# Nine matmuls on a zeroed tile at the start, and all tables loaded on the SP queue, in a two-layer encoder trunk

## The chip, the cores and the metric

The kernel runs on one core of a Trainium2 chip. The metric is the device time of one launch in microseconds. Engines work side by side, each with its own queue in order: PE multiplies matrices, PEld is its weight load, DVE and ACT work elementwise, POOL and SP mostly issue DMAs here. DMAs can be issued from SP, ACT and POOL.

## What is computed

Two layers over x (512 positions of 1024 channels, float32), then a final RMSNorm:

```python
for l in range(DEPTH):
    h = rms_norm(x, norm1_g[l])
    za, xb, q, k, v, g = jnp.split(h @ w_in[l], splits, axis=-1)
    ya = spatial_gating(jax.nn.gelu(za), a_vnorm_g[l], a_ws[l], a_bs[l])
    yb = multiscale_pool(xb, b_w[l], b_scale[l])
    yc = retention(q, k, v, g, c_norm_g[l])
    x = x + jnp.concatenate([ya, yb, yc], axis=-1) @ w_out[l]
    x = x + conv_ffn(rms_norm(x, norm2_g[l]), w_up[l], conv_w[l], conv_b[l], w_down[l])
return rms_norm(x, final_g)
```

The retention part uses rotary tables (cos, sin), a decay mask over pairs of positions and decay factors by head; the spatial gating uses a 128x128 weight per head with a block mask and a bias; the pooling uses one weight per group, its window counts and a selector.

## The kernel before

x stands transposed, eight tiles X[k] of 128 channels x 512 positions. Every float32 operand of a large matmul is split in two float32r halves, a rounded one (h) and the rest (l), and a product is three matmuls: h x h, h x l, l x h. ACT writes the h half (a cast or a scaled copy), DVE the l half (a subtraction).

The weights are cut on the host into 192 slots of 128 x 1024, 96 per layer, in the order in which PE uses them. The class Weights loads them on the SP queue into a ring of five raw tiles (wr) and splits them into rings of five tiles (wh, wl). The first four slots come in halves of 256 KB, each followed by one x row (Weights.first, lines 65 to 78); the others are single loads of 512 KB (line 83), asked for three slots ahead of use (line 91).

load_x (line 710) loads X[k] on SP and calls Norm.feed (line 171): a copy of the row scaled by the norm's gain (ACT, n_kh), its rest (DVE, n_kl), its square (ACT, n_kq) and the running sum of squares (DVE, into n_0q). For k = 0 a small square root follows, which brings an activation table load. The gains are columns of the vector table vecs; ACT's queue loads its first eight columns at k = 0 and the others at k = 3.

In mixing (line 246) the first projection is token_proj for the values, slots 0 to 3. Each x row k is one block of 12 matmuls: four groups of 128 positions, each h x h, h x l, l x h in that order (lines 241 to 243), so that the third matmul of a block is the first that needs n_kl. Before the last block the hook puts in the statistics (n_0ss: matmuls of the summed squares with ones), and behind the first two rows of the query projection (slot 4) the spreading of the norm factor (n_0rb). The order in which the many small steps of mixing are written out is the string MIX; the queues of all engines are ordered by a planner when the program is built, which may pull an instruction ahead of others of its engine.

The tables: selt, cntt, dmt, dect and epst (lines 133 to 143), loaded once, and wst, bit, bwt, cos and sin (lines 254 to 263), loaded for each layer, all issued from POOL. cos and sin take tiles from the ring U of 48 general tiles; wst, bit and bwt have one tile each, which layer 1 gets when layer 0 is done with it. Their first readers are late in the layer, but for dect and cos, which are read when the norm factor is there.

The up projections of layer 0's ffn end with slot 84, and slot 85 is the first of its last down projection.

Of the kernel before, what the change touches and what calls it, by code (L numbers as in the profile page):

```python
# [10 lines left out]
F32 = mybir.dt.float32  # L11
F32R = mybir.dt.float32r
# [4 lines left out]
P = 128  # L17
# [3 lines left out]
KT = D // P  # L21
NT = T // P
AW = 256
CW = 512
HEADS = 8
# [14 lines left out]
SLOTS_PER_LAYER = 96  # L40
LOOK = 3
FIN = 2
MIX = (
    "Q0 K0 v23 G0 v01 Q1 s0 K1 G1 s1 y0 Q2 s2 y1 K2 s3 B0 y2 Q3 s4 y3 K3 "
    "m0 r01 s5 y4 A s6 G2 y5 G3 s7 y6 y7 r2 c1 c0 B1 r3 a U1 c2 c3 m1 U0"
# [2 lines left out]
SLOT = {}  # L48
for _n in MIX:
    if _n[0] in "QKGBUA":  # L50
# [48 lines left out]
def trunk(ctx: ExitStack, tc: tile.TileContext, xT, wflat, vec, ws_t, bias_t, bw, rope, dmask, vdec, geps, cnt, sel, out):  # L99
    nc = tc.nc  # L100
    cp = ctx.enter_context(tc.tile_pool(name="const", bufs=1))
    lp = ctx.enter_context(tc.tile_pool(name="layer", bufs=1))
# [6 lines left out]
    def U(name, dt=F32, cols=T):  # L109
        return up.tile([P, cols], dt, tag="u", name=name)  # L110

    def PS(name):
        return psp.tile([P, T], F32, tag="ps", name=name)

    def f(ap):
        return ap.bitcast(F32)
# [9 lines left out]
    vecs = cp.tile([P, NV], F32, name="vecs")  # L126
# [4 lines left out]
    eps = cp.tile([P, 1], F32, name="eps")  # L131
    nc.vector.memset(eps, EPS)
    selt = cp.tile([P, 2], F32, name="selt")
    nc.gpsimd.dma_start(out=selt, in_=sel)
    cntt = cp.tile([P, 2, 17], F32, name="cntt")
    nc.gpsimd.dma_start(out=cntt, in_=cnt)

    dmt = cp.tile([P, HEADS, P], F32, name="dmt")
    nc.gpsimd.dma_start(out=dmt, in_=dmask)
    dect = cp.tile([P, NT, HEADS], F32, name="dect")  # L140
    nc.gpsimd.dma_start(out=dect, in_=vdec)
    epst = cp.tile([P, 4, NT, 2], F32, name="epst")
    nc.gpsimd.dma_start(out=epst, in_=geps)

    def rsqrt(src, n, scale, name, eps_t=None):
        m = sp.tile([P, n], F32, tag="rm", name=name + "m")
# [99 lines left out]
    def mixing(l, nm, nxt):  # L246
# [5 lines left out]
            return vecs[:, vc + c : vc + c + 1]  # L252

        wst = lp.tile([P, 4, P], F32, tag="wst", name=f"wst{l}")
        nc.gpsimd.dma_start(out=wst, in_=ws_t[l])
        nc.gpsimd.memset(wst[CHUNK:P, :, 0:CHUNK], 0.0)
        bit = lp.tile([P, 2, P], F32, tag="bit", name=f"bit{l}")
        nc.gpsimd.dma_start(out=bit, in_=bias_t[l])
        bwt = lp.tile([P, 2, P], F32, tag="bwt", name=f"bwt{l}")
        nc.gpsimd.dma_start(out=bwt, in_=bw[l])  # L260
        cosr, sinr = U(f"cos{l}"), U(f"sin{l}")
        nc.gpsimd.dma_start(out=cosr, in_=rope[0])
        nc.gpsimd.dma_start(out=sinr, in_=rope[1])

        vb = token_proj(f"v{l}_", base, 4, CW, hs, ls, nm.stats)
        V = []
# [264 lines left out]
        def step(name):  # L531
            kind, i = name[0], [int(c) for c in name[1:]]
            if kind == "Q":
                q(i[0])
            elif kind == "K":
                k(i[0])
            elif kind == "G":
                gate(i[0])
            elif kind == "v":
                v_center(i)  # L540
            elif kind == "s":
                scores(i[0])
            elif kind == "y":
                ymix(i[0])
            elif kind == "r":
                yvar(i)
            elif kind == "c":
                ycat(i[0])
            elif kind == "A":
                state["va"] = va_begin()  # L550
            elif kind == "B":
                state[i[0]] = pool(i[0])
            elif kind == "m":
                poolmap(i[0], state[i[0]])
            elif kind == "a":
                state["sg"] = spatial(state["va"])
            elif kind == "U":
                acat(i[0], state["sg"][i[0]])

        for name in MIX:  # L560
            step(name)

        ch, cl = [c[0] for c in cat], [c[1] for c in cat]
        place = {"c": 4, "m": 2, "U": 0}
        order = [place[n[0]] + int(n[1]) for n in MIX if n[0] in place]
        banks = {}
# [66 lines left out]
    def finish(s, G):  # L633
        def down(m, c, n, hook=None):
            ps = PS(f"fd{m}_{c.start}")[:, : c.stop - c.start]
            for k in range(FH):
                if k == 4 and hook is not None:
                    hook()
                i = m * FH + k
                mm3(ps, W.get(s + i // KT), i % KT, G[k][0][:, c], G[k][1][:, c], k == 0, k == FH - 1)  # L640
            nc.vector.tensor_tensor(out=X[m][:, c], in0=X[m][:, c], in1=ps, op=ALU.add)
            sq = U(f"fq{m}_{c.start}")[:, : c.stop - c.start]
            nc.scalar.activation(out=sq, in_=X[m][:, c], func=AF.Square)
            return sq
# [3 lines left out]
        nc.scalar.activation(out=warm, in_=total[:, :1], func=AF.Sqrt)  # L648
        for m in range(1, KT - FIN):
            sq = down(m, slice(0, T), T)  # L650
            nc.vector.tensor_tensor(out=total, in0=total, in1=sq, op=ALU.add)
        r = {}
        for th in range(2):
            c = slice(th * H, (th + 1) * H)
            part = total[:, c]
            for m in range(KT - FIN, KT):
                hook = None
                if th == 1 and m == KT - FIN:
                    sums = [part0, sq]
# [4 lines left out]
                sq = down(m, c, H, hook)  # L664
                if th == 1 and m == KT - FIN:
                    fin_out(0, r[0])
# [19 lines left out]
    def fin_out(th, r):  # L686
        rb = PS(f"frb{th}")
        for b in range(NT // 2):
            nc.tensor.matmul(
                rb[:, b * P : (b + 1) * P], r[:, b : b + 1].to_broadcast([P, P]), ident, start=True, stop=True  # L690
            )
        c = slice(th * H, (th + 1) * H)
        for k in range(0, KT, 2):
            o = U(f"fin{th}_{k}")
            for i in range(2):
                nc.vector.scalar_tensor_tensor(
                    out=o[:, i * H : (i + 1) * H],
                    in0=X[k + i][:, c],
                    scalar=vecs[:, C_FG + k + i : C_FG + k + i + 1],
                    in1=rb[:, :H],  # L700
                    op0=ALU.mult,
                    op1=ALU.mult,
                )
            (nc.sync if k % 4 else nc.scalar).dma_start(
                out=out[th, :, k : k + 2, :], in_=o.rearrange("p (a t) -> p a t", a=2)
            )
# [3 lines left out]
    def load_x(k):  # L710
        xt = cp.tile([P, T], F32, name=f"x{k}")
        nc.sync.dma_start(out=xt, in_=xT[k])
        if k == 0:
            nc.scalar.dma_start(out=vecs[:, :8], in_=vec[:, :8])
        if k == 3:
            nc.scalar.dma_start(out=vecs[:, 8:], in_=vec[:, 8:])
        X.append(xt)
        nm.feed(k)

    W.first(load_x)  # L720
    for l in range(DEPTH):
        n2 = Norm(f"n2_{l}", l * LC + C_N2)
        mixing(l, nm, n2)
        nm = Norm(f"n1_{l + 1}", (l + 1) * LC + C_N1) if l < DEPTH - 1 else None
        ffn(l, n2, nm)
# [106 lines left out]
```

## Time and profile before

| | us |
|---|---|
| median of three runs | 1141.26 (1140.46 to 1141.29) |
| span of the profiled execution, first to last instruction | 1139.3 |
| PE busy | 1125.2 (99%) |
| DVE busy | 746.4 (66%) |
| ACT busy | 525.1 (46%) |
| POOL busy | 27.5 (2%) |

The busy time of PE counts matmuls from start to a modelled end, so that it says where PE stands idle, not how fast it goes; how fast it goes is read from the distance between the starts of matmuls. The chain of work that ended last names, from the end back to the start, what each step waited for. The granted clock of PE is 0.998 of full speed as a mean of the span; the two levels are 1.2 and 2.4 GHz. Queue q1 is SP's, q10 ACT's and q0 POOL's.

### The profile page before, as it was taken

Reading aid. Unit: us, or ns where it says so; the run is one execution under the profiler, and the core shown is the slowest. Engines: PE = TensorE matmul, PEld = TensorE weight load, DVE = VectorE, ACT = ScalarE, POOL = GpSimd, SP = SyncE. Lnnn points to the kernel's source line nnn. Section 1 sums busy time; section 2 is a strip of 40 time slices with the busy share of each in tenths; the row PEclk is TensorE's granted clock in tenths of the full one; section 3 lists DMA queues with packets and bytes.
Section 4 is the critical chain, followed back from the end, with each engine's and each line's share of the span. In section 5 each row is a group of like instructions: output and inputs, shape, how many; then the busy total and the mean of one; then the engine's idle time right before and its main releaser. Section 6 shows DMA issues by size and latency. Waiting matters only on the chain.

```text
span 1139.3 us, 13715 instructions
## 1 busy us (share of the span) xinstructions
PE 1125.2 (99%) x5378; PEld 941.7 (83%) x5378; DVE 746.4 (66%) x1103; ACT 525.1 (46%) x731; POOL 27.5 (2%) x71
## 2 busy tenths in 40 slices
PE   8999999999999999999999999999999999999997
PEld 6888888888888888888888898888888888888886
DVE  6898676576763377764448877666777435777534
ACT  7577745444431244444327785534444213444420
POOL 2010000000000000000001000000000000000000
PEclk9999999999999999999999999999999999999999
DMA  9433222233223222233224322222232223322202
GB/s 326 146 111 93 75 75 96 90 102 102 93 93 101 103 93 93 97 105 113 93 93 123 100 74 71 78 93 93 96 107 94 93 96 106 95 93 93 93 1 74
DMA packets 33361, 112.83 MB, mean 99 GB/s; under 512 B 4320, under 2 KB 4496, under 8 KB 33296
## 3 DMA queue, kind: packets, MB, share of 16 engines
q1 hardware_dynamic: 29952, 103.82, 27.1%
q0 software_dynamic: 2480, 6.87, 2.3%
q10 hardware_dynamic: 864, 1.26, 0.3%
q8 instruction: 42, 0.69, 0.2%
q14 instruction: 23, 0.19, 0.0%
HBM read 105.64 MB, written 2.10 MB: 95 GB/s over the span
## 4 chain that ended last, share of the span: by engine, by line
PE 99%; DVE 0%; DMA 0%; ACT 0%; issue 0%; DVEq 0%; SPq 0%; ACTq 0%
PE up L214 14%; PE up L212 14%; PE up L213 14%; PE dn L214 5%; PE dn L213 5%; PE dn L212 5%; PE o L212 3%; PE o L214 3%; PE o L213 3%; PE fd L212 2%; PE fd L213 2%; PE fd L214 2%; PE v L241 1%; PE v L242 1%; PE v L243 1%; PE k L213 1%
## 5 line engine op out<-in xcount | busy, mean ns | idle before, releaser
L86 ACT CAST wh<-wr 128x1024 fp32r<-128x1024 f32 x188 | 197.7, 1052 | 291.7 <-PE dn L213 104.2
L87 DVE TENSOR_TENSOR wl<-wr,wh 128x1024 fp32r<-128x1024 f32 x188 | 229.8, 1223 | 106.0 <-ACT wh L86 103.1
L610 DVE SCALAR_TENSOR_TENSOR cc<-uu,vecs,cc 128x511 f32<-128x511 f32 (+1 forms) x176 | 131.4, 748 | 5.4 <-ACT cc L606 2.3
L606 ACT ACTIVATE cc<-uu,vecs 128x512 f32<-128x512 f32 x88 | 71.5, 815 | 7.9 <-DVE uu L604 7.7
L614 ACT ACTIVATE cc<-cc 128x512 f32<-128x512 f32 x44 | 27.8, 632 | 79.0 <-DVE cc L610 79.0
L604 DVE TENSOR_TENSOR uu<-up,n_1bc 128x512 f32<-128x512 f32 x44 | 30.2, 688 | 40.9 <-PE up L214 40.9
L604 DVE TENSOR_TENSOR uu<-up,n_0bc 128x512 f32<-128x512 f32 x44 | 30.2, 688 | 40.9 <-PE up L214 40.9
L626 DVE TENSOR_TENSOR x<-x,dn 128x512 f32<-128x512 f32 x24 | 16.5, 687 | 40.9 <-PE dn L214 40.9
L212 PE MATMUL up<-n_0h,wh 128*128 128x512 f32 x88 | 34.7, 394 | 0.0
L213 PE MATMUL up<-n_0l,wh 128*128 128x512 f32 x88 | 34.3, 390 | 0.0
L214 PE MATMUL up<-n_1h,wl 128*128 128x512 f32 x88 | 34.3, 390 | 0.0
L212 PE MATMUL up<-n_1h,wh 128*128 128x512 f32 x88 | 34.3, 390 | 0.0
L212 PE MATMUL up<-n_3h,wh 128*128 128x512 f32 x88 | 34.3, 390 | 0.0
L214 PE MATMUL up<-n_5h,wl 128*128 128x512 f32 x88 | 34.3, 390 | 0.0
L214 PE MATMUL up<-n_2h,wl 128*128 128x512 f32 x88 | 34.3, 390 | 0.0
L212 PE MATMUL up<-n_7h,wh 128*128 128x512 f32 x88 | 34.3, 390 | 0.0
L213 PE MATMUL up<-n_4l,wh 128*128 128x512 f32 x88 | 34.3, 390 | 0.0
L213 PE MATMUL up<-n_6l,wh 128*128 128x512 f32 x88 | 34.3, 390 | 0.0
L213 PE MATMUL up<-n_5l,wh 128*128 128x512 f32 x88 | 34.3, 390 | 0.0
L214 PE MATMUL up<-n_6h,wl 128*128 128x512 f32 x88 | 34.3, 390 | 0.0
L214 PE MATMUL up<-n_3h,wl 128*128 128x512 f32 x88 | 34.3, 390 | 0.0
L212 PE MATMUL up<-n_4h,wh 128*128 128x512 f32 x88 | 34.3, 390 | 0.0
(959 smaller groups left out, 3058.3 us busy)
## 6 DMA issues: line engine op xcount, KB each, us to landing
wr<-in_wflat_dram SPq DMA_DIRECT2D x188, 512.0 KB, 3.5
wr<-in_wflat_dram SPq DMA_DIRECT2D x8, 256.0 KB, 7.3
x<-in_xT_dram SPq DMA_DIRECT2D x8, 256.0 KB, 7.8
qs_0h<-qs_0h POOLq DMA_DIRECT2D x8, 128.0 KB, 2.3
qs_1h<-qs_1h POOLq DMA_DIRECT2D x8, 128.0 KB, 3.7
qs_0l<-qs_0l POOLq DMA_DIRECT2D x8, 128.0 KB, 3.4
qs_1l<-qs_1l POOLq DMA_DIRECT2D x8, 128.0 KB, 3.8
out_dram<-fin ACTq DMA_DIRECT2D x4, 256.0 KB, 2.2
```

The lines of the kernel that those rows point to most:

```text
L86: nc.scalar.copy(hi, src)
L87: nc.vector.tensor_tensor(out=lo, in0=src, in1=hi.bitcast(F32), op=ALU.subtract)
L212: nc.tensor.matmul(ps, hi[:, k, :], xh, start=first, stop=False)
L213: nc.tensor.matmul(ps, hi[:, k, :], xl, start=False, stop=False)
L214: nc.tensor.matmul(ps, lo[:, k, :], xh, start=False, stop=last)
L241: nc.tensor.matmul(o, hs[k][:, bs], hi[:, kk, :], start=k == 0 and b % pack == 0, stop=False)
L242: nc.tensor.matmul(o, hs[k][:, bs], lo[:, kk, :], start=False, stop=False)
L604: nc.vector.tensor_tensor(out=u, in0=ps, in1=nm.bc, op=ALU.mult)
L606: nc.scalar.activation(out=c, in_=u, func=AF.Identity, scale=w[2], bias=vecs[:, vc + C_CB + t : vc + C_CB + t + 1])
L610: nc.vector.scalar_tensor_tensor(out=c[:, d:], in0=u[:, : T - d], scalar=w[2 - d], in1=c[:, d:], op0=ALU.mult, op1=ALU.add)
L614: nc.scalar.activation(out=c, in_=c, func=AF.Silu)
L626: nc.vector.tensor_tensor(out=X[m], in0=X[m], in1=ps, op=ALU.add)
```

## The change

A tile of 128 x 512 is zeroed by DVE, and nine matmuls of its first 128 columns with the whole tile write a PSUM tile that nothing reads. The DMAs of all tables go from POOL to SP: the five that are loaded once stand in layer 0 behind cos and sin, and so behind the 16 weight and x rows of Weights.first. The order within a layer is now cos, sin, (the five), bwt, bit, wst. The larger part of vecs goes from ACT at the fourth x row to SP at the last.

```diff
+WARM = 9
@@
     selt = cp.tile([P, 2], F32, name="selt")
-    nc.gpsimd.dma_start(out=selt, in_=sel)
     cntt = cp.tile([P, 2, 17], F32, name="cntt")
-    nc.gpsimd.dma_start(out=cntt, in_=cnt)
-
     dmt = cp.tile([P, HEADS, P], F32, name="dmt")
-    nc.gpsimd.dma_start(out=dmt, in_=dmask)
     dect = cp.tile([P, NT, HEADS], F32, name="dect")
-    nc.gpsimd.dma_start(out=dect, in_=vdec)
     epst = cp.tile([P, 4, NT, 2], F32, name="epst")
-    nc.gpsimd.dma_start(out=epst, in_=geps)
+
+    zero = U("zero", F32R)
+    nc.vector.memset(f(zero), 0.0)
+    busy = PS("busy")
+    for i in range(WARM):
+        nc.tensor.matmul(busy, zero[:, :P], zero, start=True, stop=True)
+
+    def load_tables():
+        for t, src in ((dect, vdec), (selt, sel), (cntt, cnt), (epst, geps), (dmt, dmask)):
+            nc.sync.dma_start(out=t, in_=src)
@@
         wst = lp.tile([P, 4, P], F32, tag="wst", name=f"wst{l}")
-        nc.gpsimd.dma_start(out=wst, in_=ws_t[l])
+        bit = lp.tile([P, 2, P], F32, tag="bit", name=f"bit{l}")
+        bwt = lp.tile([P, 2, P], F32, tag="bwt", name=f"bwt{l}")
+        cosr, sinr = U(f"cos{l}"), U(f"sin{l}")
+        nc.sync.dma_start(out=cosr, in_=rope[0])
+        nc.sync.dma_start(out=sinr, in_=rope[1])
+        if l == 0:
+            load_tables()
+        nc.sync.dma_start(out=bwt, in_=bw[l])
+        nc.sync.dma_start(out=bit, in_=bias_t[l])
+        nc.sync.dma_start(out=wst, in_=ws_t[l])
         nc.gpsimd.memset(wst[CHUNK:P, :, 0:CHUNK], 0.0)
-        bit = lp.tile([P, 2, P], F32, tag="bit", name=f"bit{l}")
-        nc.gpsimd.dma_start(out=bit, in_=bias_t[l])
-        bwt = lp.tile([P, 2, P], F32, tag="bwt", name=f"bwt{l}")
-        nc.gpsimd.dma_start(out=bwt, in_=bw[l])
-        cosr, sinr = U(f"cos{l}"), U(f"sin{l}")
-        nc.gpsimd.dma_start(out=cosr, in_=rope[0])
-        nc.gpsimd.dma_start(out=sinr, in_=rope[1])
@@
-        if k == 3:
-            nc.scalar.dma_start(out=vecs[:, 8:], in_=vec[:, 8:])
+        if k == KT - 1:
+            nc.sync.dma_start(out=vecs[:, 8:], in_=vec[:, 8:])
```

## Rows read from the trace of the kernel before

**Rows 1.** Waits of PE: waiter, releaser: us in total, times, longest.

```profile
PE v L241 <- ACT n_0h L176: 5.6, 1, 5.6
PE frb L689 <- DVE fr1r L162: 1.3, 1, 1.3
```

**Rows 2.** The chain that ended last, its start: start us, us, what.

```profile
1.19 3.55 DMA x<-in_xT_dram
4.82 0.73 ACT n_0h L176
5.60 0.80 PE v L241
...
10.23 0.43 PE v L242
...
10.93 0.23 PE v L241
```

**Rows 3.** Stretches: length, busy (instructions) by engine, granted clock, DMA share, GB/s.

```profile
5.60:10.60 5.00, 5.00 (x12) 3.86 (x13) 2.17 (x3) 3.44 (x6) 0.68 (x5) 1.00 1.00 348
10.60:16.00 5.40, 5.40 (x25) 4.46 (x24) 4.41 (x7) 4.68 (x9) 1.37 (x3) 1.00 1.05 382
```

**Rows 4.** Timeline of PE: start us, us, line, operation [idle before <- releaser].

```profile
6.19 0.63 PE L242 MATMUL v<-wl,n_0h 128*128 128x512 f32 x1
...
13.98 0.39 PE L243 MATMUL v<-wh,n_2l 128*128 128x512 f32 x1
...
27.13 0.95 PE L193 MATMUL n_0ss<-ones,n_0q 128*128 128x1 f32 x8
...
30.80 0.39 PE L212 MATMUL q<-n_0h,wh 128*128 128x512 f32 x1
...
507.63 0.39 PE L212 MATMUL dn<-G_11h,wh 128*128 128x512 f32 x1
```

**Rows 5.** Timeline of DVE.

```profile
0.84 0.06 DVE L132 MEMSET eps<- 128x1 f32 x1
...
12.27 0.75 DVE L177 SCALAR_TENSOR_TENSOR n_2l<-x,vecs,n_2h 128x512 fp32r<-128x512 f32 x1
...
25.33 0.69 DVE L187 TENSOR_TENSOR n_0q<-n_0q,n_7q 128x512 f32<-128x512 f32 x1
...
56.58 0.17 DVE L368 MEMSET sc<- 128x128 f32 x1
```

**Rows 6.** DMA queues, 2 to 4 us (q10), then 6 to 12 us.

```profile
q10 hardware_dynamic: 229, 0.14, 23.3%
...
q1 hardware_dynamic: 590, 1.08, 52.4%
q0 software_dynamic: 407, 1.09, 49.5%
```

**Rows 7.** Timeline of ACT.

```profile
8.28 0.72 ACT L176 ACTIVATE n_1h<-x,vecs 128x512 fp32r<-128x512 f32 x1 [0.97 <-DMA x<-in_xT_dram]
9.02 1.28 ACT L185 ACT_TABLE_LOAD   x1
...
14.57 0.60 ACT L75 CAST wh<-wr 128x512 fp32r<-128x512 f32 x1
...
16.22 0.60 ACT L75 CAST wh<-wr 128x512 fp32r<-128x512 f32 x1
...
21.63 1.05 ACT L86 CAST wh<-wr 128x1024 fp32r<-128x1024 f32 x1 [0.18 <-DMA wr<-in_wflat_dram]
...
23.12 0.71 ACT L176 ACTIVATE n_7h<-x,vecs 128x512 fp32r<-128x512 f32 x1
```

**Rows 8.** Timeline of POOL, the table loads of layer 1.

```profile
149.40 0.57 POOL L255 DMA_DIRECT2D wst<-in_ws_t_dram  x1 [43.79 <-PE sg L500]
...
512.73 0.54 POOL L262 DMA_DIRECT2D cos<-in_rope_dram  x1 [354.19 <-DVE cc L616]
513.76 0.54 POOL L263 DMA_DIRECT2D sin<-in_rope_dram  x1 [0.50 <-DVE G_21l L122]
```

**Rows 9.** Timeline of SP, 0 to 512.7 us: the weight loads in it.

```profile
14.26 496.01 SPq L83 DMA_DIRECT2D wr<-in_wflat_dram  x91
```

**Rows 10.** DMA issues on the page: KB each, median us to landing.

```profile
wr<-in_wflat_dram SPq DMA_DIRECT2D x188, 512.0 KB, 3.5
```

## The prediction

> **What bounds the kernel now.** I read the waits of the PE first: it waited 5.6 us for its first operand and after that only at the very end [rows 1]. Everything between is one line of matmuls, and the page gives the chain of the end 99% to PE. So a change pays only by what it takes off PE's own line, and here that is the start. Second, the chain from time zero [rows 2]: weight row, x row (landed at 1.19 + 3.55 = 4.74), ACT's scaled copy, first projection matmul at 5.60. The next matmuls on the chain stand 0.43 us apart up to 10.23 and 0.23 us apart from 10.93. In the table of stretches twelve matmuls lie between 5.60 and 10.60, twenty-five between 10.60 and 16.00 [rows 3]. The fine paces: 0.427 us slow, which is 512 columns at the 1.2 GHz level, and 0.227 fast (58 matmuls from 13.98 to 27.13 [rows 4]). The clock column says 1.00 in both stretches, but the pace is nearly halved. I trust the pace and put the rise at 10.55, that is 4.95 us after PE's first matmul. Third, how late PE is against its supply in the first projection: the third matmul of a block needs the low half of x (n_kl on DVE), and it runs 0.96 us after that for block 2 (12.27 + 0.75 = 13.02 against 13.98 [rows 4, 5]); the stats matmuls at 27.13 run 1.1 us after their sum (25.33 + 0.69 = 26.02 [rows 4, 5]).
>
> **The change, step by step.** Its own time is the span, 1139.3 us; the median of the runs, 1141.26, lies 1.96 us above it, and I carry that over.
>
> *Nine matmuls added.* They need only a DVE memset of 128x512, behind two small ones that end at 0.90 [rows 5]. Its price is not in the trace: below, a 128x128 memset took 0.17 us, above, a DVE pass over 128x512 took 0.69 [rows 5]. From 0.06 for one column and 0.17 for 128 I estimate 0.06 + 511 x 0.11/127 = 0.50 us, so it ends near 1.4 and the first added matmul starts there. In the profile the second matmul starts 0.59 after the first (6.19 against 5.60), the others 0.43 apart [rows 2, 4]. Nine at the slow pace occupy PE to 1.4 + 0.59 + 8 x 0.427 = 5.4. That is idle time of PE until 5.60 [rows 1]; what is left of it is what matters. If the memset takes 0.69, they end at 5.6 and delay nothing against before.
>
> *First real operand.* In 2 to 4 us ACT's queue (q10, the rest of the vector table) had 23.3% of the DMA time [rows 6]. Moved behind the x rows, it frees up to 0.23 x 2 = 0.5 us: x row 0 lands near 4.25 and the first real matmul could start at 5.05 to 5.60. It stands behind the nine until 5.4, so I take 5.4: 0.2 us earlier.
>
> *The clock.* If the rise comes 4.95 us after the first matmul as in this profile, it comes at 1.4 + 4.95 = 6.35. From 5.4 to 6.35 some 2.2 real matmuls are slow instead of 12. Each slow one costs 0.427 - 0.227 = 0.20. Block 0 (12 matmuls) ends at 5.4 + 12 x 0.227 + 2.2 x 0.20 = 8.6. Before, it ended at 10.7 [rows 2]. Gain 2.1 us. Bounds: rise before 5.0, block 0 from 5.1 (with 0.2 lost to n_0l) ends at 8.0, gain 2.7; rise two us later than I put it, four more slow matmuls, gain 1.3; no earlier rise than 10.55, gain 0.2.
>
> *The tables leave POOL's queue.* In 6 to 12 us they (q0) had 49.5% of the DMA time and SP's rows 52.4% [rows 6]. ACT waited for x row 1 until 8.28 [rows 7]. Behind the rows, 256 KB each take about 0.67 us at 385 GB/s (382 between 10.6 and 16 [rows 3]): row 1 lands near 4.25 + 2 x 0.67 = 5.6, row 7 near 13.6. Then ACT and DVE set the supply: ACT's passes for one row take 1.65 us (from the weight cast at 14.57 to the next at 16.22), and an activation table load of 1.28 stands before block 2's copy [rows 7]. Row 0's copy ends near 5.0; one round later, with 0.5 allowed for landings, n_1h is there at 7.15 and, with DVE's 0.75 [rows 5], n_1l at 7.9, against the third matmul of block 1 at 8.6 + 0.45 = 9.05. The table load and another round give n_2h at 10.1 and n_2l at 10.9, against 11.8. PE needs 2.72 per block, ACT 1.65, so the margin grows. Without this move the early clock would be worth only the 0.96 us of margin above: both parts are needed.
>
> *What the move puts on SP.* Eleven more issues before slot 4 (the first 512 KB load), at most the 0.57 us that an issue on POOL took [rows 8], 6 us in all, and some 1.8 MB, 4.7 us at 385 GB/s, which run at the same time. Slot 4 is used by the query projection at 30.80 [rows 4]; 6.5 MB up to and with it take 17 us at 382 GB/s; from a first landing near 3 that is 20, so this is hidden. Of the tables, dect and cos are read first, behind the statistics at 27.13, so later than slot 4 lands; dmt first by the score stage, whose memset stands at 56.58 [rows 4, 5]. ACT loses one issue and POOL ten; PE, which waited for nothing between [rows 1], did not wait for them either. POOL's memset of wst waits longer; behind it on POOL stand only the copies of the first query tile, which come after the projection that starts at 30.80.
>
> *Layer 1.* Five issues now stand between weight loads on SP, where before POOL waited 354.19 us for cos and 43.79 us for wst [rows 8]. SP had issued 91 loads (slots 4 to 94) by 512.7, while PE was in slot 85 [rows 4, 9]: nine slots, some 49 us, of cover. I cost it at nothing; without cover see the last rival.
>
> Sum: -0.2 (start) - 1.9 (ten slow matmuls at 0.20, less rounding) = -2.1: span 1137.2, time 1139.2. PE has no wait after 5.60 that could swallow it before the tail [rows 1], and the tail moves with it.
>
> **The rivals.**
>
> *The rise comes early.* The clock is up before the first real matmul: no slow ones are left, gain 2.7, 1138.6. For it: nothing shows that the delay of 4.95 us is fixed. Against: it is the only delay this trace shows. The Trainium skill ("TensorE: Matmul & The Clock Gate", section "What's actually happening") says that one kernel showed 6, 11 and 14 slow matmuls at its start in different runs. No two profiles here show that; by it the gain would scatter to both sides of mine. It would also make the time before scatter, and the three runs do, by 0.8 us.
>
> *The nine do not lift the clock earlier*, because zeros or the gap to real work leave it down until about 10.5 us: 12 x 0.427 from 5.4 ends at 10.5, gain 0.2, 1141.1. Nothing in the profile speaks for it but that no matmul on zeros is in it.
>
> *A new wait in the supply.* ACT and DVE work in a fixed order, and so far ACT's cast of slot 4 (21.63) stands ahead of its copy of x row 7 [rows 7]. If that order stays and slot 4 lands no earlier, the stats sum is ready at 26.02 as before, PE waits there, and of the gain 1.1 is left: 1140.2. Against: the row pace on the queue rises once the tables are out. The Trainium skill ("DMA: Bandwidth & Descriptors", section "Issuing engines are not separate DMA queues") says that DMAs from SP, ACT and POOL interleave on the same 16 engines and that spreading them saves only issue time. By that rule the move wins no bandwidth, only order, and total bytes ahead of slot 4 are what they were: its time would be this rival's 1140.2. The shares of [rows 6] agree with the interleaving; the pace from 5.6 to 10.6 us, 348 GB/s against 382 after it [rows 3], says that a little can be won.
>
> *SP stuck on a table (slower).* Place: the load of layer 1's cos on SP. On POOL it waited for a late gate product of layer 0 until 512.73, and sin until 513.76 [rows 8]. If the order puts it right behind the load of slot 84, the last up projection, slot 85's load starts at 514.3, lands 3.5 later [rows 10], and is cast and split in 1.05 and about as much again [rows 7]: ready at 519.9, while PE reached slot 85 at 507.63 [rows 4]. That is 12.3 us, 1151.5 with the gain. Each load that stands ahead of it takes one slot of PE off, 24 x 0.227 = 5.44; with three or more it costs nothing. SP's loads run nine ahead, so I hold it unlikely.
>
> **How the numbers follow.** My forecast 0.50 (1138.7 to 1139.9), early rise 0.22, no lift 0.12, new wait 0.10, SP stuck 0.06. The likeliest is 1139.2. A measurement of this kernel can tell about 0.2%, 2.3 us, from no change: the early rise and a third of my own case lie beyond it (0.22 + 0.16 = 0.38), the rest of mine, no lift and new wait within it (0.34 + 0.22 = 0.56), slower 0.06. For 8 in 10 the range takes in early rise, mine and new wait, 1138.6 to 1140.2, and 0.6 us on each side, since the runs before lie 0.8 apart: 1138.0 to 1140.8.
>
> **What the profile after would show.** PE busy from about 1.4; nine matmuls on the zero tile; the first v matmul at 5.1 to 5.6; the change from 0.43 to 0.23 us steps between 5 and 8; block 1 at 8.0 to 9.4 (10.7 before); POOL's queue empty until the query copies; q1 nearly alone until 14. I am wrong on supply if PE waits for n_1l, n_2l or the stats sum between 8 and 27; wrong on cover if SP waits on DVE cc ahead of a weight load and a weight cast is then waited for by PE near 510; wrong on the clock if steps of 0.43 go on beyond 9.

## The result and the profile after

The changed kernel took 1148.15 us, median of four runs (1144.47 to 1149.87), the kernel before, run beside it, 1141.28. The ratio is 1.0058, with a 95% interval of 1.0042 to 1.0074: slower by 6.9 us, where I had said 1139.2 and at most 1140.8. The profiled execution took 1148.45, its span is 1146.7 (before 1139.3). The four lie 5.4 us apart: the fastest, 1144.47, has a mean granted clock of 0.997, as the kernel before has (0.997 to 0.998), the other three 0.992 to 0.995. What follows is read from the profiled one (0.993).

The start went nearly as the prediction put it. Timeline of PE of the kernel after (start us, us, line, operation), against [rows 2, 4]:

```profile
1.51 3.86 PE L144 MATMUL busy<-zero 128*128 128x512 f32 x9 [1.51 <-DVE zero L141]
5.52 0.50 PE L246 MATMUL v<-wh,n_0h 128*128 128x512 f32 x1
5.85 0.39 PE L247 MATMUL v<-wl,n_0h 128*128 128x512 f32 x1
...
8.38 0.40 PE L246 MATMUL v<-wh,n_1h 128*128 128x512 f32 x1
...
25.52 0.94 PE L198 MATMUL n_0ss<-ones,n_0q 128*128 128x1 f32 x8
...
58.62 0.39 PE L217 MATMUL g<-n_0h,wh 128*128 128x512 f32 x1
...
98.87 0.39 PE L217 MATMUL k<-n_0h,wh 128*128 128x512 f32 x1
...
113.63 0.41 PE L246 MATMUL va<-wh,n_0h 128*128 128x256 f32 x1
...
128.12 0.40 PE L217 MATMUL g<-n_0h,wh 128*128 128x512 f32 x1
```

The same points of the kernel before:

```profile
60.23 0.39 PE L212 MATMUL g<-n_0h,wh 128*128 128x512 f32 x1
...
97.84 0.40 PE L212 MATMUL k<-n_0h,wh 128*128 128x512 f32 x1
...
108.50 0.28 PE L241 MATMUL va<-wh,n_0h 128*128 128x256 f32 x1
...
121.29 0.40 PE L212 MATMUL g<-n_0h,wh 128*128 128x512 f32 x1
```

Statistics at 25.52 instead of 27.13 [rows 4], and still 1.61 us ahead at the first gate projection (58.62 against 60.23). Then PE loses 2.64 us up to the last key projection (98.87 against 97.84), 4.10 more up to the za projection (113.63 against 108.50), and 1.70 up to the next gate projection (128.12 against 121.29). -1.61 + 2.64 + 4.10 + 1.70 = 6.83, of 7.4 in the span; the other 0.6 comes behind PE's last wait, at the very end. All of the 6.83 lies in layer 0's mixing, where the change touches no arithmetic at all.

Waits of PE after (waiter, releaser: us in total, times, longest), against [rows 1]:

```profile
PE sc L368 <- DVE S_0l L123: 2.0, 1, 2.0
PE busy L144 <- DVE zero L141: 1.5, 1, 1.5
...
PE y L393 <- DVE S_1l L123: 0.9, 1, 0.9
...
PE y L388 <- ACT S_1h L122: 0.3, 1, 0.3
PE sc L368 <- PE q L219: 0.3, 1, 0.3
```

The 5.6 us wait of [rows 1] is gone, and four waits of the score stage are new. (In the retention's score stage PE multiplies the rotated queries qs_ with the keys into sc, ACT and DVE split the masked scores into S_0 to S_2, and PE multiplies these with the values into y.) The longest is at 107.5, and it is not the whole price. Stretches of the kernel after (length, busy and instructions of PE, PEld, DVE, ACT and POOL, granted clock, DMA share, GB/s):

```profile
110.00:111.00 1.00, 1.00 (x7) 0.78 (x6) 1.00 (x3) 0.00 (x0) 0.00 (x0) 0.82 1.06 336
111.00:112.00 1.00, 1.00 (x7) 1.00 (x6) 0.30 (x1) 0.60 (x2) 0.00 (x0) 0.50 0.43 102
...
116.00:117.00 1.00, 1.00 (x6) 1.00 (x6) 0.97 (x2) 0.97 (x2) 0.00 (x0) 0.50 0.00 0
117.00:118.00 1.00, 1.00 (x9) 1.00 (x8) 0.70 (x3) 0.80 (x2) 0.00 (x0) 0.77 0.00 0
```

Some 1 us after PE went on, the granted clock fell to 0.50, the 1.2 GHz level, for six whole stretches and parts of two: 0.18 + 6 x 0.50 + 0.23 = 3.4 us lost. The kernel before has 1.00 in 110 to 120 in the same view. So the two last losses, 5.8 us, are a 2.0 us wait, 3.4 us of slow clock behind it and 0.4 that I have not placed. The fall is not of one size in every execution: the profile lost 7.7 us to the clock in all, 4.3 of them behind 1136 us, and a mean of 0.997, as in the fastest execution, leaves 4.0 at most. That one can have had little of the fall in the score stage; no trace of it was kept.

Where the wait comes from is seen on DVE. First the kernel after, then the kernel before (timeline of DVE, the same work):

```profile
104.45 0.69 DVE L321 TENSOR_TENSOR rq_3t<-rq_3t,rq_3w 128x512 f32<-128x512 f32 x1
105.85 1.23 DVE L88 TENSOR_TENSOR wl<-wr,wh 128x1024 fp32r<-128x1024 f32 x1 [0.71 <-PE bm L483]
106.99 0.68 DVE L340 TENSOR_TENSOR qs_0l<-rq_3t,qs_0h 64x512 fp32r<-64x512 f32 x1
...
108.75 0.69 DVE L123 TENSOR_TENSOR S_0l<-sc,S_0h 128x512 fp32r<-128x512 f32 x1
```

```profile
101.32 0.68 DVE L314 TENSOR_TENSOR rq_3t<-rq_3t,rq_3w 128x512 f32<-128x512 f32 x1
...
102.76 0.68 DVE L333 TENSOR_TENSOR qs_0l<-rq_3t,qs_0h 64x512 fp32r<-64x512 f32 x1
...
104.19 0.69 DVE L122 TENSOR_TENSOR S_0l<-sc,S_0h 128x512 fp32r<-128x512 f32 x1
...
105.45 1.23 DVE L87 TENSOR_TENSOR wl<-wr,wh 128x1024 fp32r<-128x1024 f32 x1
```

The instructions are the same, their order is not: the split of the 20th weight slot (wl) stood behind S_0l and S_1l, and now stands ahead of qs_0l and S_0l, where it also waits 0.71 us itself. It is not the whole delay: the last rotary pass (rq_3t) is already 3.1 us later than before, while PE's last key projection starts only 1.0 later (98.87 against 97.84). S_0l reads the scores out of PSUM and so frees the tile that PE's third score matmul needs, here that matmul in both (timeline of PE, after and before):

```profile
109.50 0.39 PE L368 MATMUL sc<-qs_1h,ks 128*128 128x256 f32 x1 [1.98 <-DVE S_0l L123]
```

```profile
105.91 0.28 PE L361 MATMUL sc<-qs_1h,ks 128*128 128x256 f32 x1
```

The 2.64 us lost before begin in the same way: at 65.27 another slot's split (1.22 us) now stands between S_0l and S_1l, and the wait of 0.9 us at 67.01 follows. The two of 0.3 come at 73.68 and 76.14, in the next score stage; 1.1 of the 2.64 I have not placed.

Up to 122 us, in layer 0's mixing, the planner that builds the queues has put instructions of DVE, ACT and PE in another order in many places; behind that, the orders of the two kernels agree. SP's queue does not stand as the program's text has it either: the five tables and bwt are issued ahead of cos (15.57) and sin (16.12). Neither DVE nor ACT waits for a DMA between 100 and 110 us.

### The profile page after: what moved, and what is told of

Its sections match the earlier page's. It is cut to its first block, busy times and chain, and to the rows that moved or that the text cites. A ratio compares the mean times of both kernels' runs of the same rounds, so it can differ in the third digit from the quotient of the medians.

```text
span 1146.7 us, 13719 instructions
## 1 busy us (share of the span) xinstructions
PE 1132.8 (99%) x5387; PEld 944.9 (82%) x5387; DVE 746.4 (65%) x1104; ACT 524.6 (46%) x731; POOL 19.4 (2%) x56
## 4 chain that ended last, share of the span: by engine, by line
PE 96%; DVE 1%; ACT 1%; DMA 0%; issue 0%; SPq 0%; DVEq 0%; ACTq 0%
PE up L217 14%; PE up L219 14%; PE up L218 14%; PE dn L219 5%; PE dn L217 5%; PE dn L218 5%; PE o L217 3%; PE o L218 3%; PE o L219 3%; PE fd L217 2%; PE fd L219 2%; PE fd L218 2%; PE k L218 1%; PE k L217 1%; PE k L219 1%; PE v L248 1%
## 5 line engine op out<-in xcount | busy, mean ns | idle before, releaser
L87 ACT CAST wh<-wr 128x1024 fp32r<-128x1024 f32 x188 | 197.7, 1052 | 293.9 <-PE dn L218 104.2
L217 PE MATMUL up<-n_2h,wh 128*128 128x512 f32 x88 | 34.3, 389 | 0.0
L219 PE MATMUL up<-n_0h,wl 128*128 128x512 f32 x88 | 34.3, 389 | 0.0
L218 PE MATMUL up<-n_2l,wh 128*128 128x512 f32 x88 | 34.2, 389 | 0.0
L218 PE MATMUL up<-n_3l,wh 128*128 128x512 f32 x88 | 34.2, 389 | 0.0
L219 PE MATMUL up<-n_4h,wl 128*128 128x512 f32 x88 | 34.2, 389 | 0.0
```

The source lines that it names most:

```text
L87: nc.scalar.copy(hi, src)
L217: nc.tensor.matmul(ps, hi[:, k, :], xh, start=first, stop=False)
L218: nc.tensor.matmul(ps, hi[:, k, :], xl, start=False, stop=False)
L219: nc.tensor.matmul(ps, lo[:, k, :], xh, start=False, stop=last)
```

## The experiments

Three theories: **order** (the new order of instructions in layer 0's mixing costs the time, whatever moved the DMAs), **transfers** (the DMAs on SP bring weights late), **clock** (the nine matmuls or the early rise are paid back by a later fall).

### The changed kernel in the order of the kernel before

All transfers and the nine matmuls are the changed kernel's; each instruction of DVE, ACT and PE, up to where the two orders agree, is chained to the one ahead of it in the order that the kernel before has on its engine. Chained instructions all carry the line of the helper that records them (L86 or L87).

```diff
+def force_order(tc, nc):
+    info = mybir.DependencyInfo(mybir.DependencyClass.NoSync, mybir.DependencyReason.DATA)
+    for name, text in ORDER.items():
+        log = getattr(nc, name).log
...
+        for i, j in zip(idx, idx[1:]):
+            tc.add_manual_dep(log[j], log[i].name, info, reason="issue order")
...
         ffn(l, n2, nm)
+    force_order(tc, nc)
```

> The changed kernel, all its transfers and the nine matmuls kept, but DVE, ACT and PE are held to the order of instructions that the planner gave the kernel before. Theory 'order' (the loss comes from the new order of weight splits and score splits in layer 0's mixing): the waits of PE on S_0l and S_1l are gone and the gain of the start shows, 1139.2 us, between 1138.5 and 1140. Theory 'transfers' (the tables on SP bring weights or tables late, and the order follows from nothing): still 1146 to 1150. Theory 'clock' (the early rise is paid back by a later fall, whatever the order): 1145 or more.

Measured: 1140.96 us (1139.60 to 1144.32, ten runs), ratio to before 1.0004, interval 0.9995 to 1.0014. The loss is gone. All of PE's waits of half a microsecond and more in it:

```profile
PE busy L208 <- DVE zero L205: 1.5, 1, 1.5
PE frb L86 <- DVE fr1r L86: 1.3, 1, 1.3
PE fss L86 <- ACT fq L86: 0.6, 1, 0.6
```

But the gain of the start is not in the median: the profiled execution took 1139.60, the ten runs scatter over 4.7 us above it, and the median lies 1.4 above. The slowest, 1144.32, has a mean clock of 0.994, the other nine 0.996 to 0.998, so a part of that one's loss seems to be slow clock; it has no trace. The profiled one's trace shows a place where hardly any margin is left: ACT waits for slot 4, with x row 7's copy queued behind, and the last sum of squares ends at 24.77 + 0.69 = 25.46; PE's statistics matmuls start at 25.52. Rows of ACT and of DVE:

```profile
21.07 1.05 ACT L86 CAST wh<-wr 128x1024 fp32r<-128x1024 f32 x1 [2.80 <-DMA wr<-in_wflat_dram]
```

```profile
24.77 0.69 DVE L86 TENSOR_TENSOR n_0q<-n_0q,n_7q 128x512 f32<-128x512 f32 x1
```

### The kernel before in the order of the changed kernel

The same helper, the other way round: tables on POOL, no added matmuls, the changed kernel's order.

```diff
+ORDER = {
...
+    force_order(tc, nc)
```

> The kernel before, tables on POOL and no added matmuls, but DVE, ACT and PE are held to the order of the changed kernel. Theory 'order': the loss comes without any transfer moved: about 7 us over the changed kernel's gain, 1148 to 1151, with PE waiting for S_0l or S_1l between 60 and 110 us. Theory 'transfers': 1141.3 as before. Theory 'clock': 1141.3 as before.

Measured: 1148.40 us (1147.98 to 1149.45), ratio 1.0069 (1.0054 to 1.0084). The new waits are there to the tenth, with no table on SP and no matmul added:

```profile
PE sc L86 <- DVE S_0l L86: 2.0, 1, 2.0
...
PE y L86 <- DVE S_1l L86: 0.9, 1, 0.9
```

The granted clock in 110 to 120 is 0.66 here, as after. This kernel has not the changed kernel's 1.6 us at the start, yet its median lies only 0.25 above; the four runs of the changed kernel lie 5.4 us apart, too wide to tell that. This kernel and the first experiment's both carry the chains, so these are not the cause. So the order alone makes the loss; transfers and clock fall as causes of it, and the fall of the clock comes with the order's waits, as a part of what the order costs.

### Each half of the change alone

Nine matmuls alone, tables left on POOL:

```diff
+WARM = 9
...
+    zero = U("zero", F32R)
+    nc.vector.memset(f(zero), 0.0)
+    busy = PS("busy")
+    for i in range(WARM):
+        nc.tensor.matmul(busy, zero[:, :P], zero, start=True, stop=True)
```

> The kernel before with the nine matmuls alone; the tables stay on POOL and the rest of the vectors on ACT, and the planner's order stays that of before. Theory 'order': no loss; the gain is held to the 0.96 us by which n_2l was ahead, so 1140.3 (1139.8 to 1140.8), with PE waiting for the x rows in the first 15 us. Theory 'transfers': the same. Theory 'clock': 1145 or more.

Measured: 1140.19 us (1139.62 to 1140.93), ratio 0.9994 (0.9985 to 1.0003): 0.9 us, which the interval does not tell from nothing, and less than the nine can give. The supply is as late as before: the last sum of squares ends at 25.49 + 0.69 = 26.18, and PE's statistics start at 26.23. PE also waits for its first row behind the nine:

```profile
PE v L248 <- ACT n_0h L183: 0.8, 1, 0.8
```

Tables alone, no matmuls:

```diff
-    zero = U("zero", F32R)
-    nc.vector.memset(f(zero), 0.0)
-    busy = PS("busy")
-    for i in range(WARM):
-        nc.tensor.matmul(busy, zero[:, :P], zero, start=True, stop=True)
```

> The changed kernel without the nine matmuls: tables and the rest of the vectors on SP; the planner's order is nearly that of the changed kernel. Theory 'order': the loss is here, and the first projection starts slow: 1148 to 1151. Theory 'transfers': the same. Theory 'clock': about 1141.

Measured: 1148.97 us (1148.20 to 1150.11), ratio 1.0073 (1.0058 to 1.0088), with the long wait of the changed kernel:

```profile
PE sc L362 <- DVE S_0l L123: 2.0, 1, 2.0
```

So the move of the tables brings the new order, the nine matmuls don't. Why the planner orders otherwise when these DMAs are issued from SP can't be read from a trace and stays open.

### One swap made, and one undone

Is the 20th slot's split enough? First in the good order of the first experiment: only this slot's cast and split move ahead of qs_0 and S_0.

```diff
-... 106-109 128 110 ...
+... 128 106-110 ...
...
-... 151 142-143 145 147 173 150 ...
+... 151 173 142-143 145 147 150 ...
```

(128 is ACT's cast, 173 DVE's split; 106 to 109 and 142 to 147 are the qs_ and S_ passes.)

> The first experiment's kernel (order of the kernel before) with one thing moved: the cast and the split of one weight slot, the 20th, stand ahead of the score stage's qs_0 and S_0 passes of the last query tile of layer 0, where the changed kernel has them. The cast can start only when the third key projection has let go of the buffer, so S_0l ends 2.5 to 3.1 us later than there, and PE's third score matmul, which had 1.0 us of margin, waits 1.5 to 2.1 us near 104.5. Theory (one wait, then the clock): behind that wait stand small matmuls, the granted clock falls to 0.50 for some 7 us as in the changed kernel, and the kernel comes to 1145.5 to 1147.5, 5 to 6 us above the first experiment. Rival (the wait alone): 1142.3 to 1143.2, with a clock of 1.00 throughout 100 to 120 us. Rival (the many small moves together are needed): no wait over 0.5 us, 1140.5 to 1141.5.

Measured: 1146.48 us (1143.26 to 1147.61), 5.5 above the first experiment. PE's waits and the stretches where the clock falls:

```profile
PE n_0ss L86 <- DVE n_0q L86: 2.3, 1, 2.3
PE sc L86 <- DVE S_0l L86: 1.6, 1, 1.6
```

```profile
108.00:109.00 1.00, 0.91 (x6) 0.74 (x7) 1.00 (x3) 0.04 (x1) 0.12 (x1) 0.90 0.95 336
109.00:110.00 1.00, 1.00 (x5) 0.90 (x4) 0.70 (x2) 0.21 (x1) 0.00 (x0) 0.50 1.02 348
```

One moved split of 1.23 us becomes 1.6 us of wait and 3.4 of slow clock (0.10 + 6 x 0.50 + 0.31 up to 116). The wait and the clock are as the theory has them. That the median lies in its range is in part luck. The other line, 2.3 us for the sum of squares, was not expected here: it is the place with little margin of the first experiment, and in this execution slot 4 landed 2 us later still. This profile lies 6.9 us above the first experiment's (1146.48 against 1139.60), of which the swap has 5.0 and the sum 2.3. And the five executions lie 4.4 us apart, with mean clocks of 0.993 to 0.996: the fall is not of one size in them either.

Then the reverse: the changed kernel in its own order, with only this split put back behind S_0 and S_1.

```diff
-... 102-105 128 106-110 ...
+... 102-109 128 110 ...
...
-... 173 142 164 143 145 147 166 150 ...
+... 142 164 143 145 147 173 166 150 ...
```

> The changed kernel in its own order, but for one thing: the cast and the split of that one weight slot, the 20th, stand behind qs_0 and S_0, S_1 of the last query tile, where the kernel before has them. Theory (one wait, then the clock): the 2.0 us wait of the third score matmul near 107.5 shrinks under 0.7 us, the granted clock stays at 1.00 from 105 to 120 us, and the kernel comes to 1142 to 1143.5, some 5 to 6 us under the changed kernel; what is left is the 2.3 us lost between 60 and 77 us. Rival (the wait alone): 1145.8 to 1146.5. Rival (other moves put the wait there as well): 1147.5 to 1149, with the wait still at 1.5 us or more.

Measured: 1146.36 us (1144.91 to 1148.36), 1.8 under the changed kernel, not 5 to 6, and the two kernels' executions overlap. The wait is still there:

```profile
PE sc L87 <- DVE S_0l L87: 1.5, 1, 1.5
```

and the clock stands at 0.50 from 108 on. DVE tells why; first this kernel, then the one with the swap made, at the rotary step that starts the last query tile:

```profile
99.60 0.68 DVE L87 TENSOR_TENSOR rq_3t<-q,cos 128x512 f32<-128x512 f32 x1
...
101.37 1.23 DVE L87 TENSOR_TENSOR wl<-wr,wh 128x1024 fp32r<-128x1024 f32 x1
```

```profile
97.66 0.68 DVE L86 TENSOR_TENSOR rq_3t<-q,cos 128x512 f32<-128x512 f32 x1
```

In the new order the rotary step itself comes 1.9 us later, behind other passes of DVE, and it leads to qs_0 and S_0 as well. So one swap is enough to make the wait near 107 us and the slow clock behind it, but it is not the only thing that makes them: the new order has a second path to the same wait. The theory falls. The rival that other moves put the wait there too holds by the wait (1.5 us), though its time, 1147.5 or more, is above the median; the median lies in the range of the wait alone, but here the clock fell with the wait.

### A version that keeps the gain

First step: the first experiment, with slot 4's cast and split behind the passes for x row 7.

```diff
-... 24 17 19 25 20 22 26 23 27 29 28 ...
+... 24 17 19 20 22 23 25 26 27 29 28 ...
...
-... 24-25 20 22-23 26-27 33 28-32 36 ...
+... 24 20 22-23 25-27 33 28-32 36 ...
```

(25 to 27 and 33 are the casts and splits of slots 4 to 7, 20 and 22 and 23 the passes for rows 6 and 7, 28 to 32 the statistics.)

> The changed kernel in the order of the kernel before, as in the first experiment, but ACT's cast and DVE's split of weight slot 4 stand behind the passes for x row 7 on their engines. In the first experiment ACT waited 2.80 us at 21.07 for slot 4 to land, ahead of the copy of row 7, and the sum of squares was ready at 25.46 with PE's first statistics matmul at 25.52. Theory (supply): that near-zero margin is where the 1.5 us gained at the start are lost again in some executions, so here the sum is ready 1.5 to 2.5 us earlier, PE has no wait but 1.5, 1.3 and 0.6, and the median comes to 1138.5 to 1139.9. Rival (nothing in the supply): the executions of the first experiment differ for another reason, and the median stays at 1140.5 to 1141.5. Rival (slot 4 too late): the query projection at 29.2 waits for slot 4's split, 0.5 to 2 us, 1141 to 1142.5.

Measured: 1140.74 us (1139.99 to 1141.47, eleven runs), ratio 0.9997 (0.9988 to 1.0006). The spread shrank from 4.7 us to 1.5, as the supply theory has it (without the slowest execution of the first experiment it was 3.3), and the sum of squares is ready at 20.67; the median did not fall by more than the scatter. There is a new wait, one step on:

```profile
PE n_0rb L86 <- DVE n_0r L86: 1.2, 1, 1.2
```

```profile
27.54 2.50 DVE L86 TENSOR_TENSOR wl<-wr,wh 128x1024 fp32r<-128x1024 f32 x2 [0.94 <-ACT wh L86]
29.96 0.15 DVE L86 TENSOR_SCALAR n_0m<-n_0ss 128x4 f32<-128x4 f32 x1
```

n_0m could have started behind the statistics matmuls near 25.9, but four splits stand ahead of it, and they wait for slots that land late. Second step: the statistics ahead of the splits of slots 5 to 7.

```diff
-... 25 26 27 29 28 ...
+... 25 26 28 27 29 ...
...
-... 25-27 33 28-32 36 ...
+... 25 28-32 26-27 33 36 ...
```

> The kernel of the fifth experiment (slot 4's split behind row 7) with one more move: DVE's and ACT's statistics steps (n_0m to n_0r) stand behind slot 4's split and ahead of those of slots 5 to 7. There n_0m stood behind four splits that waited for slots landing at 22.9 to 27.7, so that n_0r was ready at 31.2 and PE's n_0rb waited 1.2 us. Theory (supply): n_0r is ready near 27.5, n_0rb (near 30.0) doesn't wait, PE has no wait but 1.5, 1.3 and 0.6, and the median is 1.0 to 1.3 us under the fifth experiment's 1140.74: 1139.3 to 1139.9, faster than both kernels by 0.1 to 0.17%. Rival (slots 5 and 6 become late): their splits start at 27.5 instead of 25.2, PE needs slot 5 near 35, so a wait there is held unlikely; it would leave 1140.5 or more. Rival (the scatter between executions is not of the supply): the times still spread over 1.5 us or more and the median stays at 1140.5 to 1141.0.

Measured: 1139.67 us (1139.05 to 1140.47, eleven runs), ratio 0.9988 (0.9979 to 0.9997): faster than both kernels, if by little. n_0rb starts at 30.04 without a wait, and the waits of PE are the three that were expected.

```profile
25.00 0.95 PE L86 MATMUL n_0ss<-ones,n_0q 128*128 128x1 f32 x8
...
30.04 1.05 PE L86 MATMUL n_0rb<-ident,n_0r 128*128 128x128 f32 x8
```

Last, the same without the memset and the nine matmuls:

```diff
-    zero = U("zero", F32R)
-    tc.nc.vector.memset(f(zero), 0.0)
-    busy = PS("busy")
-    for i in range(WARM):
-        tc.nc.tensor.matmul(busy, zero[:, :P], zero, start=True, stop=True)
```

> The kernel of e9_stats_first without the memset and the nine matmuls: all tables on SP, the order of the kernel before with slots 4 to 7 split late. Theory (the clock's rise follows PE's first work): the first projection runs at 0.43 us steps until some 5 us after its first matmul at 5.1 to 5.6, the statistics matmuls start near 26.7 to 27.1, and the median is 1.3 to 2.0 us above e9_stats_first: 1141.0 to 1141.6. Rival (the tables' move alone brings the gain): within 0.5 us of e9_stats_first.

Measured: 1141.12 us (1140.30 to 1141.70), 1.45 above. Its first projection runs at 0.43 us steps up to 9.6:

```profile
5.17 0.80 PE L86 MATMUL v<-wh,n_0h 128*128 128x512 f32 x1 [5.17 <-ACT n_0h L86]
...
9.60 0.39 PE L86 MATMUL v<-wl,n_0h 128*128 128x512 f32 x1
...
26.42 0.95 PE L86 MATMUL n_0ss<-ones,n_0q 128*128 128x1 f32 x8
```

So the nine are worth 1.45 us (statistics at 25.00 against 26.42), the tables' move by itself nothing that can be measured, and both are small beside what the order can cost.

## Why the prediction was wrong

**The step that failed.** "PE has no wait after 5.60 that could swallow it before the tail [rows 1], and the tail moves with it", and, of layer 1's moved DMAs, "I cost it at nothing". Both take the order of the instructions on DVE, ACT and PE as given, and count only what the moved DMAs do at run time. In this kernel a planner draws that order when the program is built, as the description of the kernel before says, and I used its queues as if they were written by hand. [rows 1] shows that PE waited for nothing between, not how near it came: in the kernel before S_0l ended at 104.88, 1.0 us ahead of the third score matmul at 105.91. One split of 1.23 us more ahead of S_0l is over that margin: made alone, that swap cost 1.6 us of wait and 3.4 of slow clock. In the changed kernel late rotary passes lead over the margin as well, and an earlier split costs 0.9 near 67 us. No rival had this mechanism; the only slower one, SP stuck on a table of layer 1, was the wrong place.

**What was right.**
- The memset: 0.50 estimated, 0.48 measured; the first added matmul at 1.51 (1.4 predicted).
- First real matmul 5.52 (5.4); x row 0 was there at 4.74 as before, not near 4.25, and its copy was ready at 4.74 + 0.72 = 5.46, so the nine stand in idle time.
- That the nine bring the clock's rise forward: 6.35 predicted, but the steps are 0.23 us from 5.85 on, so that one real matmul at most was slow, not 2.2; this lies nearer to the rival of an early rise. Block 1 starts at 8.38 (8.0 to 9.4).
- The statistics: 25.52, 1.61 us earlier, against 1.9 + 0.2, is near by two errors that partly cancel. At block 1 the gain was 10.77 - 8.38 = 2.4 us. The supply then took 0.8 back: n_1l was ready at 8.96 and n_2l at 12.18, where I had 7.9 and 10.9, and PE's third matmuls of blocks 1 and 2 came right behind them, in steps of 0.40 and 0.51 us. "So the margin grows" was wrong, and by my own sign I was wrong on supply: x row 1 was there at 7.45, not near 5.6.
- Both parts needed: nine alone 0.9 us (not clear of the scatter), tables alone none.
- Layer 1's cover: SP waited 12.8 us for wst's tile and 3.4 for bit's, and PE waited nowhere near; the rival of SP stuck did not come.

**The rival of a new wait in the supply** (1140.2) has its place right, though not in the changed kernel, whose own order already has slot 4 behind row 7. In the order of the kernel before it came in full: PE waited 2.3 us for the sum in one profile, and moving slot 4 back took 3.2 us off the spread (1.8 without the slowest execution). "Against: the row pace on the queue rises once the tables are out" overlooked that the 1.8 MB of tables stand ahead of slot 4 on the same queue: its cast could start at 21.63 before [rows 7], and at 22.7 to 23.7 in seven of the eight traces with the tables on SP (21.07 in the first experiment's). Nor were the bytes ahead of it moved as fast: from 14 to 18 us the eight traces show 249 to 315 GB/s, the three with the tables on POOL 389 to 391. The Trainium skill ("DMA: Bandwidth & Descriptors", section "Issuing engines are not separate DMA queues") says that another issuing queue gains only issue time, usually small beside the transfer. Here it need not be small: in the changed kernel SP's issues of dect, selt, cntt and epst take from 11.50 to 14.21 us for 50 KB. That this is why the rate falls is not shown; no run moved these four alone.

## What to carry to other kernels

Where a planner orders the queues, compare the order of instructions on every engine of the two builds before any sum is made: a moved DMA can redraw it far from where it stands, and here that cost 7 us for a gain of 1.5. A row of waits that shows none is no margin; read how long ahead of its reader each releaser ends, above all where small matmuls run. And when one step is made earlier, look at once at the next producer (here the sum, then n_0r): the gain is only had when all of them lead.

## What the hardware showed

The granted clock fell to 0.50 at 107.9 to 112.6 us in the five profiles in which PE had stood idle for 1.5 to 2.0 us in the score stage (after, the kernel before in its order, the tables alone, and with the swap made or undone), and stayed there for 6 us or more: with the swap made, a wait of 1.6 us cost about 5. It did not fall after 2.3 us of idle time in the first projection (the swap's profile, at 25 us), nor after 1.2 us at 30 us (with slot 4 behind row 7). Ahead of the idle time behind which it fell PE ran the score stage's small matmuls, ahead of the other two a projection. The mean clocks of executions without a trace say that the fall is not of one size in every execution of a kernel. The Trainium skill ("TensorE: Matmul & The Clock Gate", section "A second HAM failure mode: psum-queue depth-cycling") tells of a kernel whose clock goes up and down when PE is often idle for short times between groups of matmuls. In these traces one such wait was enough, though not every one was; no run here varied what stands around it.

Matmuls on zeros brought the rise of the clock forward as matmuls on data do: in the profile of the changed kernel steps of 0.23 us begin at 5.85, behind nine matmuls on zeros and one on data; in the last experiment's, without the nine, they begin at 9.60, behind ten on data.
